# Small transfers of softmax statistics and weights: issued by GpSimd in place of SyncE

## The chip, the core and the metric

The kernel runs on one core of a Trainium2 chip. The core has five engines with an instruction queue each: TensorE (PE; its weight loads are shown as PEld), VectorE (DVE), ScalarE (ACT), GpSimd (POOL) and SyncE (SP). Every queue is worked off in order. A DMA is an instruction in the queue of some engine; it waits there for its semaphores like any other instruction, and the transfer itself is done by the core's 16 DMA engines. The metric is the device time of one execution in microseconds.

## What is computed

One layer of an encoder trunk on 1024 positions of width 1024, in float32. From the reference, cut to the part around the change:

```
hn = rms_norm(h, mix_norm_g);  proj = hn @ w_in            # q, k, v, glu, q_mem
q, k = partial_rotary(rms_norm(q)), partial_rotary(rms_norm(k))      # 8 heads x 64
for window, dil in ((128, 1), (512, 4), (2048, 16)):
    o, lse = dilated_attention(q, k, v, window, dil)
wts  = softmax(stack(lses), axis=0)
attn = sum(wts * stack(outs))
c    = silu(layer_norm(depthwise_conv31(ga * sigmoid(gg))))
mo   = cross-attention into 256 memory tokens, 4 heads x 64
h    = h + concat(attn, c, mo) @ w_out
f    = depthwise_conv3(rms_norm(h, ffn_norm_g) @ w_up);  h = h + (silu(fg) * fu) @ w_down
```

## The kernel before

Products are taken in three passes of a float32 value split into a rounded part and a rest (`w_hi`, `w_lo`), so every weight tile costs ACT a copy and POOL or DVE a subtraction (L636, L1208). The program has three stages: projections of x by `w_in` (L917, L943) with attention started beside them; the output projection by `w_out` (L1099) beside the last heads and the memory attention; and the feed-forward part (L1226, L1334). The projections come in the order q0 kv g0 g1 v0 q1 v1 q2 m q3; a projected tile of q and k is normalised and turned on POOL (`r` at L164 and L165, `t` and `raw` at L854 to L857) through four `raw` buffers.

Patterns two and three of the attention are one masked product, so a head has two groups: group 0 (window 128) and group 1 (the two dilated ones). For each head, `scores_of` (L239, L240) leaves in `stat` and `stat2` a negated maximum and a denominator for each query. Group 1 has its queries in another order, by residue class. `softmax_weights(h, ...)` brings both into one order and makes the weights of the two groups:

- L299: eight DMAs store `stat2` in scratch memory `st_d[h]`, 16 partitions of 4 pieces of 16 bytes each;
- L303, L304, L306: four DMAs load it back into `stat` in group 0's order;
- L315 to L326: POOL makes the weights `w` (ACT the exponential), TensorE turns them (L330), DVE copies them to `rows` (L333);
- L336, L337: four DMAs store `rows` in scratch memory `w_d[h]`.

`weigh(p)`, one for each pair of heads, loads each head's weights broadcast over 64 partitions into `wt` (L468, eight DMAs per pair, two `wt` buffers) and multiplies them onto the heads' outputs `u` (L480, L485). That is 20 DMAs per head and 160 in all. The values of a head are loaded at L393 and L394 into `v`, the new output's operands at L1085, projection weights at L595 and L603 (`w_raw`, two buffers, freed by the subtraction at L636).

The Python generators only say in which order work may be considered; the order on each engine is written by the scheduler of the tile framework, which plans with estimated times of its own. So an instruction that changes its engine also changes the place of others.

Of the kernel before, what the change touches and what calls it, by code (L numbers as in the profile page):

```python
# [18 lines left out]
S, D = 1024, 1024  # L19
# [113 lines left out]
def block(tc, a, out):  # L133
    nc = tc.nc
    pe, act, dve, pool, sp = nc.tensor, nc.scalar, nc.vector, nc.gpsimd, nc.sync
# [40 lines left out]
    st_d = [dpool.tile([8, 64, 2, 2], F, name=f"st_d{h}") for h in range(8)]  # L176
    w_d = [dpool.tile([1, 2, S + 64], F, name=f"w_d{h}") for h in range(8)]
    stored = {}

    def count(key):  # L180
        stored[key] = stored.get(key, 0) + 1
# [38 lines left out]
    def new_mixed(k):  # L220
        while not room_for(k):
            yield
        kind_of[k] = room_for(k)
        return (yield from st.several(2, kind_of[k], [128, S], R))

    def finish_mixed(k, parts):
        if kind_of[k] == "mx_part":
            for i, t in enumerate(parts):
                sp.dma_start(m_d[:, k, i], f32(t))
            st.free("mx_part", "mx_part")  # L230
            del kind_of[k]
            count(("mixed", k))
        else:
            mixed[k] = parts
# [54 lines left out]
    def split_mixed(k, parts, src, cut=slice(None)):  # L289
        hi, lo = (t[:, cut] for t in parts)  # L290
        act.activation(natural(hi), classed(src), AF.Copy)
        yield
        dve.tensor_tensor(natural(lo), classed(src), f32(natural(hi)), OP.subtract)

    def softmax_weights(h, stat, stat2):


        for k in range(8):
            sp.dma_start(st_d[h][k].rearrange("(r s) c n -> s r (c n)", r=4),  # L299
                         stat2[16 * k : 16 * k + 16].rearrange("s r c n -> s r (c n)"))  # L300
        yield
        there = stat[:, 1].rearrange("p u c n -> p u (c n)")
        sp.dma_start(there[0:64], st_d[h][1:8:2].rearrange("k p c n -> p k (c n)"))  # L303
        sp.dma_start(there[64:128, 0:3], st_d[h][2:7:2].rearrange("k p c n -> p k (c n)"))  # L304
        for c in range(2):
            sp.dma_start(stat[64:128, 1, 3, c], st_d[h][0, :, 1 - c])  # L306
        st.free("stat2")
        for _ in range(4):
            yield
        w = yield from st.new("w", [128, 2, 2, 4])  # L310
        wd = yield from st.new("wd", [128, 4, 2, 4])
        nm, d = (stat[:, :, :, :, i].rearrange("p g u c -> p g c u") for i in range(2))
        one = wd[:, 2]
        for g in range(2):
            pool.tensor_tensor(w[:, g], nm[:, g], nm[:, 1 - g], OP.subtract)  # L315
        yield
        act.activation(w, w, AF.Relu)
        act.activation(w, w, AF.Exp, scale=-1.0)
        yield
        for g in range(2):  # L320
            pool.tensor_tensor(wd[:, g], w[:, g], d[:, g], OP.mult)
        pool.tensor_tensor(one, wd[:, 0], wd[:, 1], OP.add)
        pool.tensor_tensor(wd[:, 3], one, expo[:, 0:1, None].to_broadcast([128, 2, 4]), OP.pow)
        pool.tensor_tensor(wd[:, 3], wd[:, 3], wd[:, 3], OP.mult)
        for g in range(2):
            pool.tensor_tensor(w[:, g], w[:, g], wd[:, 3], OP.mult)  # L326
        st.free("stat", "wd")
        yield
        ps = yield from st.new("z", [128, 512])
        pe.transpose(ps[0:16, 0:128], w.rearrange("p g c u -> p (g c u)"), ident)  # L330
        yield
        rows = yield from st.new("rows", [16, 128])
        dve.tensor_copy(rows, ps[0:16, 0:128])  # L333
        st.free("z", "w", "rows")
        for g in range(2):
            sp.dma_start(w_d[h][0, g, 64 : S + 64].rearrange("(u p) -> u p", p=128), rows[8 * g : 8 * g + 8])  # L336
            sp.dma_start(w_d[h][:, g, 0:64], rows[8 * g + 7 : 8 * g + 8, 64:128])  # L337
        count(("w", h))

    def head(h):  # L340
# [44 lines left out]
        else:  # L385
            st.kept["qk"] = 0
        st.start(softmax_weights(h, stat, stat2))
        while stored.get(("v", h // 4), 0) < NT:
            yield
# [66 lines left out]
    def weigh(p):  # L456

        for h in (2 * p, 2 * p + 1):
            while stored.get(("w", h), 0) < 1:
                yield  # L460
        parts = yield from new_mixed(p)
        wts = {}

        def fetch(half, g):

            t = wts[half, g] = yield from st.new("wt", [128, 512])
            for o in range(2):
                sp.dma_start(t[64 * o : 64 * o + 64],  # L468
                             w_d[2 * p + o][:, g, 512 * half : 512 * half + 512].to_broadcast([64, 512]))

        for g in range(2):
            yield from fetch(0, g)
        while stored.get(("u", 2 * p + 1), 0) < 4 or stored[("u", 2 * p)] < 4:
            yield
        us = joined[p]
        for half in range(2):
            cut = slice(512 * half, 512 * half + 512)
            adder = dve if p == 3 and half else pool
            for g in range(2):
                adder.tensor_tensor(us[g][:, cut], us[g][:, cut], wts[half, g], OP.mult)  # L480
                st.free("wt")
            if not half:
                for g in range(2):
                    yield from fetch(1, g)
            adder.tensor_tensor(us[0][:, cut], us[0][:, cut], us[1][:, cut], OP.add)  # L485
            yield
            yield from split_mixed(p, parts, us[0][:, cut], cut)
        st.free("u", "u")
        yield
        finish_mixed(p, parts)  # L490
# [834 lines left out]
    for part in range(2):  # L1325
        banks = [psp.tile([128, 512], F, name="ps_dn", tag=tag, bufs=n) for tag, n in DBANKS]
        for k in range(NF):
# [3 lines left out]
            for n, ps in enumerate(banks):  # L1331
                t, half = n // 2, n % 2
# [3 lines left out]
        for n, ps in enumerate(banks):  # L1336
            t, half = 4 * part + n // 2, n % 2
            r = pu.tile([128, 512], F, name="res", tag="part", bufs=6)
# [28 lines left out]
```

## Time and profile before

| what | value |
|---|---|
| median of 3 runs | 1310.53 us (1309.65 to 1312.85) |
| profiled execution, its own time | 1310.28 us |
| its span | 1308.5 us |
| mean granted TensorE clock | 0.963 |
| engine that is busy most | TensorE 91% |
| DMA queues | one hardware queue, 166460 packets, 163.63 MB, 40.3% of 16 engines |

The profile gives busy times of an engine, which do not count DMA-issuing instructions; these stand in rows of the queue (SPq, POOLq). "A <- B" in a row of waits reads: A stood idle until B was done. The chain of waits follows the execution back from its last instruction, at each step to what released it.

### The profile page before, as it was taken

What the parts mean: (1) busy time and instruction counts of PE and PEld (TensorE: products, weight loads), DVE (VectorE), ACT (ScalarE), POOL (GpSimd) and SP (SyncE); (2) the same over time, 40 slices, a digit from 0 to 9 for tenths busy, and PEclk for the clock granted to TensorE, in tenths of its full rate; (3) what the DMA queues carried; (4) which work ended last, traced back from release to release, by engine and by line L of the source; (5) the groups of instructions that cost most, each with busy time, mean ns of one, the idle gap of its engine ahead of it and who ended that gap; (6) DMA issues with size and microseconds to landing.
All of it is one profiled execution on the core that took longest, in us unless ns stands there. A gap on an engine that the chain in (4) does not pass through costs nothing.

```text
span 1308.5 us, 18556 instructions
## 1 busy us (share of the span) xinstructions
PE 1197.1 (91%) x6287; PEld 1000.3 (76%) x6287; DVE 868.7 (66%) x1272; ACT 626.6 (48%) x1296; POOL 788.5 (60%) x793
## 2 busy tenths in 40 slices
PE   4899988799988898885999999999999999999997
PEld 3887887799877786563877777777777788888886
DVE  6748879676685786887487778778787762224222
ACT  5664165468766576553344444344444443333331
POOL 4835286498894454367466667676676745555552
PEclk9999988999989898896999999999999999999999
DMA  7353525566575622161122222222222254448443
GB/s 253 112 170 100 159 82 161 169 180 178 144 252 164 188 74 78 28 213 49 34 87 81 65 86 67 81 89 65 89 71 83 81 175 155 145 145 272 146 146 120
DMA packets 166555, 164.81 MB, mean 126 GB/s; under 512 B 20322, under 2 KB 125756, under 8 KB 166460
## 3 DMA queue, kind: packets, MB, share of 16 engines
q1 hardware_dynamic: 166460, 163.63, 40.3%
q8 instruction: 49, 0.80, 0.3%
q14 instruction: 46, 0.38, 0.1%
HBM read 121.51 MB, written 42.08 MB: 125 GB/s over the span
## 4 chain that ended last, share of the span: by engine, by line
PE 46%; DVE 18%; issue 8%; ACT 7%; POOL 6%; DMA 5%; SPq 1%; POOLq 0%; ACTq 0%; DVEq 0%
PE ps_dn L1334 18%; PE ps_c L1226 6%; PE ps_d L1226 6%; PE proj L1099 4%; PE proj L917 3%; DVE yg L1295 3%; DVE conv L980 2%; DVE yu L1295 2%; PE o L287 2%; DMA v<-vr_d 2%; POOL up_lo L1208 2%; PE turn L278 2%; PE ps_a L1226 2%; ACT yu L1293 2%; DVE yg L1294 1%
## 5 line engine op out<-in xcount | busy, mean ns | idle before, releaser
L917 PE MATMUL proj<-w_hi,hnT 128*128 128x256 f32 x896 | 188.1, 298 | 23.7 <-ACT raw L832 12.9
L1208 POOL TENSOR_TENSOR up_lo<-dn_raw,up_hi 128x512 fp32r<-128x512 f32 x88 | 131.7, 1517 | 114.1 <-ACT up_hi L1207 111.3
L1208 POOL TENSOR_TENSOR up_lo<-up_sum,up_hi 128x512 fp32r<-128x512 f32 x88 | 154.8, 1768 | 55.8 <-PE ps_c L1226 22.7
L917 PEld LDWEIGHTS proj<-w_hi,hnT 128*128 128x128 f32 x896 | 150.9, 200 | 27.9 <-ACT raw L832 14.1
L1208 POOL TENSOR_TENSOR up_lo<-up_raw,up_hi 128x512 fp32r<-128x512 f32 x66 | 116.0, 1760 | 68.8 <-PE ps_a L1226 46.3
L1208 DVE TENSOR_TENSOR up_lo<-dn_raw,up_hi 128x512 fp32r<-128x512 f32 x44 | 57.6, 1311 | 147.5 <-ACT up_hi L1207 141.4
L1207 ACT ACTIVATE up_hi<-dn_raw 128x512 fp32r<-128x512 f32 x132 | 75.1, 623 | 161.4 <-issue 118.8
L1334 PE MATMUL ps_dn<-up_lo,up_hi 128*128 128x512 f32 x352 | 136.8, 389 | 0.0
L1334 PE MATMUL ps_dn<-up_hi,up_lo 128*128 128x512 f32 x352 | 136.3, 389 | 0.0
L1334 PE MATMUL ps_dn<-up_hi 128*128 128x512 f32 x352 | 134.7, 389 | 0.0
L917 PE MATMUL proj<-w_lo,hnT 128*128 128x256 f32 x448 | 131.9, 294 | 0.0
L1226 PE MATMUL ps_c<-S,up_hi 128*128 128x512 f32 x352 | 113.5, 404 | 6.6 <-ACT p L1278 6.6
L1226 PE MATMUL ps_a<-A,up_hi 128*128 128x512 f32 x352 | 111.1, 396 | 0.0
L636 POOL TENSOR_TENSOR w_lo<-w_raw,w_hi 128x512 fp32r<-128x512 f32 x44 | 62.8, 1437 | 59.4 <-ACT w_hi L634 58.8
L1221 DVE TENSOR_TENSOR up_sum<-up_raw,up_sum 128x512 f32<-128x512 f32 x40 | 59.0, 1476 | 50.4 <-POOL up_lo L1208 50.4
L917 PEld LDWEIGHTS proj<-w_lo,hnT 128*128 128x128 f32 x448 | 89.7, 200 | 0.5 <-POOL w_lo L624 0.4
L980 DVE SCALAR_TENSOR_TENSOR conv<-conv,cwT 128x1009 f32<-128x1009 f32 (+14 forms) x60 | 89.3, 1488 | 0.8
L1226 PEld LDWEIGHTS ps_c<-S,up_hi 128*128 128x128 f32 x352 | 65.4, 190 | 28.3 <-ACT p L1278 13.6
L1111 DVE TENSOR_TENSOR x<-proj,x 128x512 f32<-128x512 f32 x96 | 64.1, 682 | 25.0 <-PE proj L1099 24.9
L1293 ACT ACTIVATE yu<-cu,fwT 128x1024 f32<-128x1024 f32 x22 | 27.4, 1244 | 108.0 <-DVE cu L1286 106.3
L1226 PEld LDWEIGHTS ps_a<-A,up_hi 128*128 128x128 f32 x352 | 65.8, 188 | 15.8
L1334 PEld LDWEIGHTS ps_dn<-up_lo,up_hi 128*128 128x128 f32 x352 | 66.1, 188 | 13.8
(240 smaller groups left out, 3150.2 us busy)
## 6 DMA issues: line engine op xcount, KB each, us to landing
up_raw<-w_up SPq DMA_DIRECT2D x92, 256.0 KB
dn_raw<-w_down SPq DMA_DIRECT2D x88, 256.0 KB
g_d<-yg SPq DMA_DIRECT2D x22, 512.0 KB
dn_raw<-g_d SPq DMA_DIRECT2D x44, 256.0 KB
x<-x SPq DMA_DIRECT2D x16, 512.0 KB
qk_d<-out SPq DMA_DIRECT2D x32, 256.0 KB
qk<-qk_d SPq DMA_DIRECT2D x16, 512.0 KB
w_raw<-w_in SPq DMA_DIRECT2D x40, 128.0 KB
```

The source lines that it names most:

```text
L636: (dve if next(chunk_no) < EARLY else pool).tensor_tensor(lo, raw, f32(hi), OP.subtract)
L917: pe.matmul(ps[:, :256], lhs[i][:, k], c.parts[k][j], start=(k == 0 and i == 0 and j == 0), stop=(k == KT - 1 and i == 1))
L980: dve.scalar_tensor_tensor(acc[:, c0:c1], conv_in[i][:, c0 + k - 15 : c1 + k - 15], w, acc[:, c0:c1], OP.mult, OP.add)
L1099: pe.matmul(ps, mixed[k][i][:, 128 * t : 128 * t + 128], wo[k, half][j], start=(n == 0), stop=(n == 3 * len(ks) - 1))
L1111: dve.tensor_tensor(dst, ps, dst, OP.add)
L1207: act.activation(hi, src, AF.Copy)
L1208: adder.tensor_tensor(lo, src, f32(hi), OP.subtract)
L1221: adder.tensor_tensor(t, x, y, OP.subtract)
L1226: pe.matmul(ps, w[i][:, k], ops[x][j][:, k], start=(first and n == 0), stop=(n == 3 * KH - 1), skip_group_check=not first)
L1293: act.activation(y, c, AF.Identity, scale=tap[1], bias=b)
L1295: dve.scalar_tensor_tensor(y[:, 0 : S - 1], c[:, 1:S], tap[2], y[:, 0 : S - 1], OP.mult, OP.add)
L1334: pe.matmul(ps, gk[i][:, 128 * t : 128 * t + 128], wk[half][j], start=(k == 0 and m == 0), stop=(k == NF - 1 and m == 2))
```

## The change

Every DMA of `softmax_weights` and those of `fetch` in `weigh` are issued by POOL (`pool.dma_start`) in place of SP:

```
         for k in range(8):
-            sp.dma_start(st_d[h][k].rearrange("(r s) c n -> s r (c n)", r=4),
+            pool.dma_start(st_d[h][k].rearrange("(r s) c n -> s r (c n)", r=4),
                          stat2[16 * k : 16 * k + 16].rearrange("s r c n -> s r (c n)"))
         yield
         there = stat[:, 1].rearrange("p u c n -> p u (c n)")
-        sp.dma_start(there[0:64], st_d[h][1:8:2].rearrange("k p c n -> p k (c n)"))
-        sp.dma_start(there[64:128, 0:3], st_d[h][2:7:2].rearrange("k p c n -> p k (c n)"))
+        pool.dma_start(there[0:64], st_d[h][1:8:2].rearrange("k p c n -> p k (c n)"))
+        pool.dma_start(there[64:128, 0:3], st_d[h][2:7:2].rearrange("k p c n -> p k (c n)"))
         for c in range(2):
-            sp.dma_start(stat[64:128, 1, 3, c], st_d[h][0, :, 1 - c])
+            pool.dma_start(stat[64:128, 1, 3, c], st_d[h][0, :, 1 - c])
...
         for g in range(2):
-            sp.dma_start(w_d[h][0, g, 64 : S + 64].rearrange("(u p) -> u p", p=128), rows[8 * g : 8 * g + 8])
-            sp.dma_start(w_d[h][:, g, 0:64], rows[8 * g + 7 : 8 * g + 8, 64:128])
+            pool.dma_start(w_d[h][0, g, 64 : S + 64].rearrange("(u p) -> u p", p=128), rows[8 * g : 8 * g + 8])
+            pool.dma_start(w_d[h][:, g, 0:64], rows[8 * g + 7 : 8 * g + 8, 64:128])
...
             for o in range(2):
-                sp.dma_start(t[64 * o : 64 * o + 64],
+                pool.dma_start(t[64 * o : 64 * o + 64],
                              w_d[2 * p + o][:, g, 512 * half : 512 * half + 512].to_broadcast([64, 512]))
```

How it moves instructions shows at two places. The first is POOL's queue at the start of projection q2, where head 2's statistics (`st_d_80`) come back and pair 0's weights (`w_d_86`, `w_d_87`) are loaded. Before, from the turned tile `t_3102` to the power for `r_3071`:

```order
L856 TENSOR_TENSOR raw<-t_3102,t_3103 128x4x8
L857 TENSOR_TENSOR raw<-t_3102,t_3103 128x4x8
L164 TENSOR_SCALAR r_3071<-s_3070 128x4
L480 TENSOR_TENSOR u<-u,wt 128x512
L485 TENSOR_TENSOR u<-u 128x512
L854 TENSOR_TENSOR t_3168<-raw,rot_c 128x64
L854 TENSOR_TENSOR t_3169<-raw,rot_s 128x64
L165 TENSOR_TENSOR r_3071<-r_3071,expo 128x4
```

and in the changed program, from the same neighbourhood to the same power:

```order
L480 TENSOR_TENSOR u<-u,wt 128x512
L306 DMA stat<-st_d_80 64x2
L164 TENSOR_SCALAR r_3143<-s_3142 128x4
L306 DMA stat<-st_d_80 64x2
L856 TENSOR_TENSOR raw<-t_3102,t_3103 128x4x8
L857 TENSOR_TENSOR raw<-t_3102,t_3103 128x4x8
L304 DMA stat<-st_d_80 64x3x4
L468 DMA wt<-w_d_86 64x512
L468 DMA wt<-w_d_87 64x512
L303 DMA stat<-st_d_80 64x4x4
L165 TENSOR_TENSOR r_3071<-r_3071,expo 128x4
```

The loads of the statistics and of the weights now stand between the projection's own steps, two of them ahead of `raw` and four ahead of the power.

The second place is SP's queue around the load of the values `v` for head 6 (`st_d_84` are head 6's statistics). Before:

```order
L468 DMA wt<-w_d_90 64x512
L468 DMA wt<-w_d_91 64x512
L299 DMA st_d_84<-stat_5641 16x4x4 x6
L393 DMA v<-v_d_71 128x8x128
L394 DMA v<-vr_d_73 128x8x128
L346 DMA qk<-qk_d_69 128x1024
```

and in the changed program:

```order
L501 DMA km<-km_d 64x256
L503 DMA vm<-vm_d 128x2x128 x3
L393 DMA v<-v_d_71 128x8x128
L394 DMA v<-vr_d_73 128x8x128
L346 DMA qk<-qk_d_69 128x1024
```

The loads of weights and the stores of statistics that stood ahead of the `v` load are gone from this queue.

## The prediction

> **What bounds the kernel now.** I read the page first, then the busy times by stretch, then the chain of waits and the timelines of the two queues that exchange work.
>
> ```profile
> PE 1197.1 (91%) x6287; PEld 1000.3 (76%) x6287; DVE 868.7 (66%) x1272; ACT 626.6 (48%) x1296; POOL 788.5 (60%) x793
> ```
>
> This is the page's row for the whole span: TensorE is the bound on average. The busy times of three stretches of the attention stage, in which all moved transfers lie, show more; after the length they give PE, PEld, DVE, ACT and POOL, each with its count.
>
> ```profile
> 85.00:250.00 165.00, 145.21 (x1019) 135.17 (x1019) 132.29 (x210) 77.24 (x190) 88.00 (x103) 0.95 0.45 131
> 250.00:365.00 115.00, 103.26 (x828) 99.58 (x827) 74.31 (x193) 81.55 (x225) 95.76 (x158) 0.96 0.59 170
> 365.00:550.00 185.00, 161.37 (x892) 130.98 (x890) 139.11 (x346) 122.62 (x313) 96.25 (x147) 0.92 0.44 130
> ```
>
> The average of 60% for POOL hides that it is busy 95.76 of 115 us between 250 and 365 us, where heads 2 to 4 run beside the last three projections. Before and after that it is about half idle (88.00 of 165, 96.25 of 185). What POOL lacks in the middle stretch is this:
>
> ```profile
> POOL u L480 <- DMA wt<-w_d: 6.8, 1, 6.8
> POOL r L164 <- DVE s L838: 4.1, 4, 1.6
> POOL u L419 <- ACT u L415: 3.6, 2, 1.9
> ...
> POOL qe L353 <- PE turn L1009: 0.2, 1, 0.2
> ```
>
> These are POOL's waits from 250 to 365 us (total, times, longest). They and 115 - 95.76 = 19.2 us tell the same: 19.2 us is all the room there is. The chain of waits confirms it; from 263.5 to 290 us it runs on POOL almost without a break:
>
> ```profile
> 263.58 0.20 POOL r L164
> 263.86 0.72 POOL u L480
> ...
> 278.23 1.01 POOL qk L356
> ...
> 288.28 1.42 POOL w_lo L636
> ```
>
> So in this stretch a microsecond more on POOL is a microsecond on the path, and it is here that TensorE cannot hide it: it is itself busy 103.26 of 115.
>
> **The change part by part.** It moves 20 DMAs per head, 160 in all, from SP's queue to POOL's, and a planner places them anew among POOL's instructions. Nothing is computed more or less, and the bytes are the same. On SP their issue took (ns, least, median, most):
>
> ```profile
> L299 SPq DMA_DIRECT2D st_d<-stat x64: 302/424/1416, 97.7 to 477.1; - x64
> L306 SPq DMA_DIRECT2D stat<-st_d x16: 450/589/636, 101.3 to 475.8; - x16
> L304 SPq DMA_DIRECT2D stat<-st_d x8: 582/610/1579, 102.2 to 478.1; - x8
> L303 SPq DMA_DIRECT2D stat<-st_d x8: 591/605/2127, 102.9 to 481.5; - x8
> L468 SPq DMA_DIRECT2D wt<-w_d x32: 444/518/1608, 123.3 to 528.0; - x32
> L336 SPq DMA_DIRECT2D w_d<-rows x16: 263/269/495, 121.8 to 508.7; - x16
> L337 SPq DMA_DIRECT2D w_d<-rows x16: 214/249/253, 122.2 to 509.0; - x16
> ```
>
> By medians that is 64 x 0.424 + 16 x 0.589 + 8 x 0.610 + 8 x 0.605 + 32 x 0.518 + 16 x 0.269 + 16 x 0.249 = 71 us, or 0.44 us each, taken from SP.
>
> *Price of one on POOL.* No row shows a DMA issued by POOL. The low end is SP's 0.44 us (it cannot be a gain: an instruction on POOL takes time). The high end is the slowest thing that POOL does on a tile this small:
>
> ```profile
> L165 POOL TENSOR_TENSOR r<-r,expo 128x4 f32<-128x4 f32 x32 | 35.8, 1121 | 0.9
> L323 POOL TENSOR_TENSOR wd<-wd,expo 128x8 f32<-128x8 f32 x8 | 14.2, 1777 | 0.4
> L315 POOL TENSOR_TENSOR w<-stat 128x8 f32<-128x8 f32 x16 | 3.4, 227 | 7.1 <-DVE hl L866 6.4 <-DVE stat L239 0.6
> ```
>
> A subtraction of 128x8 takes 0.23 us, a power of the same size 1.78 us: the time goes by work per element, not by bytes. A transfer in 64 pieces (16 partitions of 4) is such work per piece. I take 1.0 us, near the power on 128x4 (1.12 us) and about the middle of 0.44 and 1.78, and keep both ends.
>
> The Trainium skill gives two figures for this and they pull apart. Its page "DMA: Bandwidth & Descriptors", section "Latency and other measured facts", puts the first byte of a DMA issued by GpSimd at about 1 us against 0.6 us from SP; an estimate from it is 1 us per DMA and the same sum as mine. The same page, section "Anatomy of one DMA — SWDGE (gpsimd) path", calls the generation of descriptors "small, variable" beside a dispatch of about 50 ns; by that the estimate would be about 0.1 us each, 56 x 0.1 = 6 us in the full stretch, and no overflow at all. No run here shows either yet; the second speaks for the faster rival below.
>
> *Stretch 250 to 365 us.* By their neighbours, 36 of the 160 stand ahead of it, 56 in it (16 with head 2's statistics and pair 0's weights, 18 and 18 with the heads after, 4 of pair 1's weights) and 68 behind. POOL would have 95.8 + 56 x 1.0 = 151.8 us of work for 115 us: 36.8 us over, called +37. Nine of the 56 stand inside the POOL chain of 263 to 290 us itself. With 0.44 us the overflow is 24.6 - 19.2 = +5; with 1.78 us it is 99.7 - 19.2 = +80. At 1.0 us nothing covers it: what waits behind is the projections' own work (r, t and raw at L164, L165, L854 to L857), whose four `raw` buffers hold TensorE back a few tiles later.
>
> *Ahead of it*, 88.0 + 36 = 124 of 165 us: hidden, cost 0, in POOL's idle 77 us; at 1.78 us it is 152, still under 165. *Behind it*, 96.3 + 68 = 164 of 185 us: the sum fits, cost 0; at 1.78 us it would be 217, or +32.
>
> *Waits that come along.* A DMA in POOL's queue holds all that stands behind it. SP paid this for the moved transfers:
>
> ```profile
> SPq L336 <- DVE rows L333: 25.5, 4, 16.1
> SPq L299 <- ACT prob L240: 8.6, 4, 5.2
> SPq L468 <- DMA w_d<-rows: 5.7, 5, 3.2
> SPq L303 <- DMA st_d<-stat: 3.9, 3, 2.7
> ```
>
> That is 43.7 us over eight heads; 56/160 of it, 15 us, falls into the full stretch, and as the planner puts other POOL work between the steps I charge a third: +5 (bounds 0 and +15). Behind such a wait stand the projections' r and raw, for which DVE and then TensorE wait.
>
> *What SP gains.* SP's queue is in order too, and the loads of the values `v` stand behind moved transfers. Head 6, then head 5:
>
> ```profile
> 434.42 1.15 PE L287 MATMUL o<-pt,v 128*128 128x256 f32 x9
> 440.04 1.09 SPq L468 DMA_DIRECT2D wt<-w_d  x2
> 441.66 3.69 SPq L299 DMA_DIRECT2D st_d<-stat  x6
> 445.44 0.38 SPq L393 DMA_DIRECT2D v<-v_d  x1
> 383.19 9.24 SPq L299 DMA_DIRECT2D st_d<-stat  x8
> 401.13 0.42 SPq L393 DMA_DIRECT2D v<-v_d  x1
> ```
>
> and, in the chain of waits, the load that follows:
>
> ```profile
> 445.92 7.02 DMA v<-vr_d
> ```
>
> The last product that read the old `v` of head 5 ended at 435.6; the load for head 6 left SP at 445.4, after transfers that now go elsewhere. Up to 10 us earlier there, and about as much at head 5 behind the 9.24 us of `st_d`. But what can be won is TensorE's idle time there:
>
> ```profile
> 390.00:455.00 65.00, 56.16 (x318) 46.22 (x316) 43.14 (x95) 41.17 (x93) 29.74 (x36) 0.97 0.60 169
> 455.00:520.00 65.00, 58.86 (x334) 48.47 (x333) 49.87 (x143) 44.39 (x127) 33.47 (x56) 0.92 0.32 85
> ```
>
> 130 - 115.0 = 15 us at most. I take 7, about half, since after the `v` load comes the next limit, VectorE's adds of the output projection.
>
> The last moved transfer starts at 528.0 us (row L468); the feed-forward part behind it has none: 0. Sum: +37 + 5 - 7 = +35. The profiled execution took 1310.28 us (span 1308.5), so 1345; the median of the runs before, 1310.53, is the same within 0.3 us.
>
> **The rivals.**
>
> *Faster: SP's relief wins (1300).* Place: the `v` loads of heads 5 and 6, 401 to 453 us. Price: -15 from the rows above, +5 for POOL at SP's own 0.44 us. It decides as soon as 56 x price - 19.2 is under 15, a price under 0.61 us; for a gain over 0.3% (4 us) under 0.54 us. For it speaks that the chain runs over DMA v<-vr_d for 7.02 us; against it, that POOL does small tiles in software times of 0.2 to 1.8 us.
>
> *Hidden (1311).* Price near 0.6 us: overflow 56 x 0.6 - 19.2 = 14, relief -14. Only a balance by chance gives it.
>
> *Slower a little (1321).* POOL at SP's price, +5, and the in-order waits, +5, with no relief because the planner leaves the `v` load behind loads of `w_raw`, which wait for POOL.
>
> *Much slower (1395).* VectorE holds POOL up while POOL writes the transfers. That such a thing exists is in the timelines:
>
> ```profile
> 260.88 2.29 DVE L980 SCALAR_TENSOR_TENSOR conv<-conv,cwT 128x1010 f32<-128x1010 f32 x1
> 262.06 1.22 POOL L856 TENSOR_TENSOR raw<-t,t 128x32 f32<-128x32 f32 x1
> 271.33 0.30 POOL L856 TENSOR_TENSOR raw<-t,t 128x32 f32<-128x32 f32 x1
> ```
>
> The same instruction takes 1.22 us under a VectorE operation with two inputs from SBUF and 0.30 us without: 0.9 us of hold. With half of the DMAs held, a mean price of 1.0 + 0.45, and with the full 15 us of waits: 56 x 1.45 - 19.2 + 15 = +77, and some of the 68 behind no longer fit: 1395. Against it: the long convolution steps end where the full stretch has hardly begun, at 264.5 us, and after them VectorE's operations of this kind are short:
>
> ```profile
> L980 DVE SCALAR_TENSOR_TENSOR conv<-conv,cwT x60: 1255/1276/2397, 108.5 to 264.5; 128x1009 f32<-128x1009 f32 x4, 128x1010 f32<-128x1010 f32 x4, 128x1011 f32<-128x1011 f32 x4, 128x1012 f32<-128x1012 f32 x4
> ```
>
> The Trainium skill has the rule on its page "SBUF — State Buffer", section "SBUF: two separate sides", in "The 'DVE blocks DMA' trap": while VectorE holds the port pair that it shares with GpSimd, GpSimd cannot write descriptors and the transfer starves. The two rows on L856 agree in kind for arithmetic; none here shows it for a DMA.
>
> **How the numbers follow.** Forecast (price 0.8 to 1.3 us, 1325 to 1372, centre 1345): 0.55. Much slower: 0.18. Faster: 0.11. Hidden: 0.08. A little slower: 0.08. The measurement tells 0.3%, about 4 us, from no change. Faster 0.11, same 0.08, slower 0.55 + 0.18 + 0.08 = 0.81. The range 1302 to 1395 leaves out about half of the faster case and half of the much slower one, 0.15 together.
>
> **What would show it.** Right: rows of POOL's queue for L299 at about 1 us; POOL without idle time from 250 to over 390 us; waits of TensorE or VectorE for POOL's r, raw or qk that are not there now; the whole feed-forward part some 35 us later, at its old pace; the `v` loads of heads 5 and 6 sooner after the last product of the head before. Wrong: DMA rows of POOL under 0.5 us, or POOL's arithmetic running on beside them; or a POOL queue that stands in waits for `st_d` and `rows`, which would put the cost in the waits and not in the issue.

## The result, and the profile after

The changed kernel took 1370.13 us in the median of 4 runs (1360.61 to 1371.22), the kernel before 1310.09 us in 4 runs beside it (1307.16 to 1312.85). The ratio is 1.0443 (95% interval 1.0391 to 1.0495): 58 us slower. Below, a cost in microseconds is always (ratio - 1) x 1311. The profiled execution took 1370.61 us, its span 1368.8 us.

The page's row for the whole span, after:

```profile
PE 1224.6 (89%) x6287; PEld 1021.3 (75%) x6287; DVE 868.6 (63%) x1272; ACT 632.6 (46%) x1298; POOL 875.4 (64%) x953
```

POOL is busy 86.9 us longer (788.5 before) and has 160 instructions more; DVE and ACT do what they did. DMAs in POOL's queue are counted as busy time, so the 86.9 us are their issue. By line, between 85 and 620 us (count, then busy us and mean ns, then the idle time ahead of them and what ended it):

```profile
L299 POOL DMA_DIRECT2D st_d<-stat x64 | 33.0, 523 | 2.0 <-ACT prob L240 1.9
L468 POOL DMA_DIRECT2D wt<-w_d x32 | 17.6, 551 | 3.1 <-PE s L258 1.1 <-POOL u L480 0.9 <-DMA w_d<-rows 0.8
L306 POOL DMA_DIRECT2D stat<-st_d x16 | 8.9, 557 | 3.3 <-DMA st_d<-stat 3.1
L336 POOL DMA_DIRECT2D w_d<-rows x16 | 8.9, 555 | 8.7 <-DVE rows L333 8.7
L337 POOL DMA_DIRECT2D w_d<-rows x16 | 8.4, 527 | 0.0
L304 POOL DMA_DIRECT2D stat<-st_d x8 | 5.3, 668 | 2.2 <-DMA st_d<-stat 2.2
L303 POOL DMA_DIRECT2D stat<-st_d x8 | 5.3, 658 | 0.1
```

Together 87.4 us, 0.55 us for each DMA (SP: 0.44), and 19.4 us of waits that they brought into the queue. The stretches of the attention stage (length, then PE, PEld, DVE, ACT and POOL busy with counts):

```profile
85.00:250.00 165.00, 142.04 (x947) 129.96 (x945) 133.03 (x193) 74.32 (x176) 101.36 (x126) 0.93 0.44 125
250.00:365.00 115.00, 94.95 (x725) 93.03 (x725) 52.68 (x151) 69.50 (x188) 99.41 (x169) 0.91 0.46 137
365.00:550.00 185.00, 150.13 (x837) 123.36 (x835) 118.73 (x302) 103.92 (x273) 133.31 (x224) 0.90 0.49 141
```

From 250 to 365 us POOL is only 3.7 us busier than before (99.41 against 95.76), although it now also issues DMAs; TensorE does 725 products in place of 828. So less work gets done in the same time. The same 6287 products also keep TensorE busy 27.5 us longer over the whole span (1224.6 against 1197.1), at a mean granted clock of 0.948 against 0.963. In the runs below that lost 20 us or more the clock was 0.942 to 0.959, in the executions of the kernel before beside them 0.959 to 0.968; no run separates what the slower products cost from the waits beside which they stand. The loss can be dated from the first and last products of two lines (the last two times are the first and the last start). The projections before, then after:

```profile
L917 PE MATMUL proj<-w_hi,hnT x896: 274/283/582, 16.4 to 370.6; 128*128 128x256 f32 x180
```
```profile
L917 PE MATMUL proj<-w_hi,hnT x896: 274/283/583, 17.0 to 404.4; 128*128 128x256 f32 x180
```

Before, the last projection product started at 370.6 us, after at 404.4: 34 us late. The first product of the feed-forward part (L1226) started at 579.0 and at 640.5 us: 62 us late, and the end is 60.3 us late. So about 34 us are lost by the end of the projections, 28 us between there and the feed-forward part, and nothing in that part.

The chain of waits shows the DMAs at the place whose order was printed above (start, length, what):

```profile
273.42 0.20 POOL r L164
273.70 1.29 POOL u L480
274.99 0.52 POOL stat L306
...
276.92 0.57 POOL stat L304
277.49 0.42 POOL wt L468
...
278.54 0.62 POOL stat L303
279.17 1.06 POOL r L165
280.25 0.44 DVE raw L860
```

Between the two halves of `r_3071`, 0.20 us and 1.06 us long, lie 5.5 us, and 3.2 us of them are DMAs of other steps (L306 twice, 0.52 and 0.58 us, L304, L468 twice, L303); DVE, then ACT and TensorE, stand behind.

### The profile page after: what moved, and what is told of

Its sections match the earlier page's. It is cut to its first block, busy times and chain, and to the rows that moved or that the text cites. A ratio compares the mean times of both kernels' runs of the same rounds, so it can differ in the third digit from the quotient of the medians.

```text
span 1368.8 us, 18618 instructions
## 1 busy us (share of the span) xinstructions
PE 1224.6 (89%) x6287; PEld 1021.3 (75%) x6287; DVE 868.6 (63%) x1272; ACT 632.6 (46%) x1298; POOL 875.4 (64%) x953
## 3 DMA queue, kind: packets, MB, share of 16 engines
q0 software_dynamic: 5632, 4.41, 1.3%
## 4 chain that ended last, share of the span: by engine, by line
PE 47%; DVE 17%; DMA 11%; ACT 8%; POOL 8%; issue 7%; SPq 1%; POOLq 0%; ACTq 0%; DVEq 0%
PE ps_dn L1334 15%; PE ps_c L1226 7%; PE ps_d L1226 6%; PE proj L917 6%; PE proj L1099 3%; PE ps_a L1226 2%; DMA w_raw<-w_in 2%; DVE yg L1295 2%; PE o L287 2%; DVE conv L980 2%; POOL up_lo L1208 2%; DMA qk<-qk_d 2%; DVE yu L1295 2%; PE ps_b L1226 2%; ACT prob L240 1%
## 5 line engine op out<-in xcount | busy, mean ns | idle before, releaser
L917 PE MATMUL proj<-w_hi,hnT 128*128 128x256 f32 x896 | 193.9, 307 | 21.2 <-DVE out L886 8.0
L917 PEld LDWEIGHTS proj<-w_hi,hnT 128*128 128x128 f32 x896 | 157.8, 210 | 25.5 <-ACT raw L832 7.0
L917 PE MATMUL proj<-w_lo,hnT 128*128 128x256 f32 x448 | 135.7, 303 | 0.5 <-POOL w_lo L624 0.5
L1226 PE MATMUL ps_c<-S,up_hi 128*128 128x512 f32 x352 | 114.1, 405 | 6.1 <-ACT p L1278 6.1
L1226 PE MATMUL ps_a<-A,up_hi 128*128 128x512 f32 x352 | 111.1, 396 | 0.0
L917 PEld LDWEIGHTS proj<-w_lo,hnT 128*128 128x128 f32 x448 | 94.2, 210 | 1.0 <-POOL w_lo L624 0.9
L1226 PEld LDWEIGHTS ps_c<-S,up_hi 128*128 128x128 f32 x352 | 65.9, 191 | 27.5 <-ACT p L1278 12.6
L1226 PEld LDWEIGHTS ps_a<-A,up_hi 128*128 128x128 f32 x352 | 65.8, 188 | 15.7
L240 ACT ACTIVATE prob<-prob,stat 128x256 f32<-128x256 f32 x128 | 63.6, 501 | 27.7 <-DVE stat L239 27.5
```

What stands on the lines that cost most here:

```text
L240: act.activation(t, t, AF.Exp, bias=nm, scale=-1.0, accum_out=den)
L917: pe.matmul(ps[:, :256], lhs[i][:, k], c.parts[k][j], start=(k == 0 and i == 0 and j == 0), stop=(k == KT - 1 and i == 1))
L1226: pe.matmul(ps, w[i][:, k], ops[x][j][:, k], start=(first and n == 0), stop=(n == 3 * KH - 1), skip_group_check=not first)
```

## The experiments

**The theories.** A: the DMAs cost what POOL loses by them, either by the time it issues them (A1, occupancy) or by the waits that come into its queue and the later landing (A2). B: the planner's new order on all queues costs, since loads now stand behind stores that wait for late POOL work. C: the old order is a lucky or picked one and any other is worse.

To hold an order, ordering edges without semaphores chain the instructions of each engine in the sequence of a table; the run under "Is it any other order?" is held in the same way and loses nothing, so the edges themselves cost no time that shows:

```
-        block(tc, aps, out)
+        block(tc, aps, out); issue_in_order(tc, nc)
...
+    for n in np.cumsum(steps.astype(np.int64)).tolist():
+        i = traced[n]
+        if n in FREE: continue
+        if i.engine in last:
+            tc.add_manual_dep(i, last[i.engine], kind, reason="order")
+        last[i.engine] = i.name
```

### Order against engine

First the changed kernel's DMAs in the old order (`ORDER_TABLE` of the kernel before, `FREE` the 160 DMAs):

> All 160 DMAs are issued by POOL, as in the changed kernel, but every other instruction of every engine is held in the order that it has in the kernel before (manual ordering edges without semaphores); only the 160 are placed freely. Theory A, occupancy and in-order waits: POOL pays 87 us of issue (0.55 us each) and the waits in its queue, whatever the order around them; the time stays near that of the changed kernel, 1355 to 1375. Theory B, the re-planned order: most of the 60 us comes from the planner's new order on the queues (loads of v, qk and w_raw behind stores that wait for late POOL work); with the old order only the overflow of the full stretch is left, 56 x 0.55 - 19.2 = 12 us less what SP gains: 1305 to 1330.

Then the reverse, the kernel before with the changed kernel's table:

> The 160 DMAs stay with SP, as before, but every other instruction of every engine is held in the order that the planner wrote for the changed kernel. Theory A, occupancy and in-order waits on POOL: without the DMAs on POOL nothing is lost, 1305 to 1320. Theory B, the re-planned order: the order costs by itself, 1340 to 1370, and the old order's loss on POOL of the first run and this one together make about the 60 us.

Measured: 1371.14 us, ratio 1.0437 (1.0403 to 1.0472), and 1364.24 us, ratio 1.0391 (1.0352 to 1.0431). Each part alone costs nearly the whole, 57 and 51 us, and both together 58. So theory A was right on the first run and missed the second, and theory B the other way round. In the old order the cost shows as waits for POOL: who waited for it from 250 to 430 us (total, times, longest),

```profile
DVE raw L860 <- POOL r L165: 23.9, 6, 12.5
ACT mx_part L291 <- POOL u L485: 22.9, 3, 15.2
...
DVE s L838 <- POOL r L164: 12.2, 2, 8.8
```

and in the kernel before, in the same window:

```profile
DVE raw L860 <- POOL r L165: 4.5, 5, 1.9
...
ACT mx_part L291 <- POOL u L485: 1.9, 3, 1.0
```

In the changed kernel itself, in the same window, the first of these rows has grown far less:

```profile
DVE raw L860 <- POOL r L165: 8.6, 5, 4.0
```

There the other engines follow an order in which they stand less behind POOL and are no faster for it. The second run shows that this order costs by itself:

```profile
250.00:365.00 115.00, 94.18 (x724) 92.08 (x723) 57.19 (x158) 69.12 (x191) 74.94 (x127) 0.90 0.45 131
```

POOL is relieved, 74.94 us busy where the changed kernel has 99.41, and yet TensorE does 724 products, one fewer than there. So an order planned for POOL as the planner estimated it keeps the slow pace when POOL is relieved, and the two 50s are not two causes that add up. The reading that fits both runs is that the one is the loss and the other its imprint on the plan; which places of that order lose the time no run shows.

### Is it any other order?

The kernel before, with the table that the planner writes when its estimate for a DMA on SP is 615 in place of 625 ns:

> The kernel before with all DMAs on SP; only the order differs: it is the one that the planner writes when its estimate for a DMA on SP is lowered by 10 of 625 ns. Nothing on the chip has another price. Theory C, tuning: the order of the kernel before is a picked one, any other costs tens of microseconds: 1325 to 1365. Theory B, the order matters only as it follows POOL's lateness: 1305 to 1318.

1311.43 us, ratio 0.9979 (0.9955 to 1.0002): no loss. By the two traces at least 1185 of TensorE's 6287 places hold a product of another line or tile, and it does not matter. Theory C fell, as far as one other order can tell.

### The planner's price

The changed kernel in the order that results from a lower estimate for POOL's DMAs:

> The changed kernel, all 160 DMAs on POOL, in the order that the planner writes when its own estimate for the issue of a DMA on POOL is lowered from 0.99 to 0.45 us, near the 0.55 us measured (0.44 us was SP's). Theory B, the order: part of the 60 us comes from planning with the wrong price, and 1325 to 1350 results. Theory A, occupancy: the work on POOL is the same, and the time stays at 1360 to 1375. Theory C, tuning: any order other than the one of the kernel before is worse, since that one was picked for this program; the result lies anywhere from 1335 to 1375, whatever the price.

1348.43 us, ratio 1.0292 (1.0267 to 1.0317), 38 us. So some 20 us of the changed kernel's 58 go with an order planned with nearly twice the measured price; 38 us stay with an order planned near it (0.45 against 0.55 us). Theory A missed here, and B's and C's ranges both hold the result; C fell by the run before. With one order for each price, the 20 us are what these two orders differ by, and not a proof that the price alone makes them.

### Occupancy or waits

Spare work in POOL's queue at the places of the DMAs, while SP issues them:

```
+    def after_spare(*move): pool.tensor_tensor(spare, half, half, OP.mult); pool.tensor_tensor(spare, half, half, OP.mult); sp.dma_start(*move)
...
-            sp.dma_start(st_d[h][k].rearrange("(r s) c n -> s r (c n)", r=4),
+            after_spare(st_d[h][k].rearrange("(r s) c n -> s r (c n)", r=4),
```

> The kernel before, every instruction in its old order and all DMAs on SP; ahead of no DMA anything waits anew. Added are 320 spare multiplications of 128x12 on POOL, two (estimated at 0.25 us each from L315, 0.23 us on 128x8) at each of the 160 places where POOL issues a DMA in the first run; they read a constant and nobody reads them. So POOL loses about the issue time of the DMAs, but waits for nothing and SP keeps its queue. If POOL's lost time is the cost (theory A1, occupancy): 1355 to 1370. If it is the waits that the DMAs bring into POOL's queue, and their later landing (theory A2): 1312 to 1330.

1361.27 us, ratio 1.0390 (1.0365 to 1.0415), 51 us. The spare row, between the first and the last of its 320:

```profile
L166 POOL TENSOR_TENSOR spare<-expo 128x12 f32<-128x12 f32 x320 | 83.0, 259 | 22.7
```

83.0 us of work that nobody needs, against 87 us of DMA issue, reproduces 51 of the 57 us. By the two traces POOL carries out the same sequence as in the first run, with two spare instructions in the place of each DMA. A1 holds: time taken on POOL is enough to make nearly the whole loss in the old order. What is left for the DMAs' waits, their landing and SP's relief together is 6 us, with intervals that touch; it isn't resolved.

### Which DMAs cost

Two kernels with one kind each on POOL, in the order that the planner writes for each (the edit is the change's own, of the lines named):

> Only the statistics' DMAs (L299, L303, L304, L306; 96 of the 160, 52.5 of the 87.4 us of issue in the changed kernel) go to POOL; the weights' stay with SP; the planner writes the order anew. If the cost goes by issue time on POOL, 52.5/87.4 of 60 us: 1346. If it goes by the waits in the queue (about 7 of the 17 us that the moved DMAs wait on POOL are the statistics'), 1335. If the order decides, no rule gives the number; it may be anything from 1305 to 1370, and not the sum with the next run.

> Only the weights' DMAs (L336, L337, L468; 64 of the 160, 34.9 of the 87.4 us of issue) go to POOL; the statistics' stay with SP; the planner writes the order anew. By issue time 34.9/87.4 of 60 us: 1334, and this gain over the kernel before plus that of the run before make 60. By order: anything from 1305 to 1370, not additive.

1341.98 us, ratio 1.0219 (1.0189 to 1.0249), 29 us; and 1333.66 us, ratio 1.0149 (1.0119 to 1.0178), 20 us. They stand 60 to 40, as the issue times do (52.5 to 34.9), and sum to 48 of 58. Both orders were planned anew, so this agrees with a cost by issue time and doesn't prove it.

Then three kernels by place, in the old order, for instance

```
-            sp.dma_start(st_d[h][k].rearrange("(r s) c n -> s r (c n)", r=4),
+            (pool if h in (2, 3, 4) else sp).dma_start(st_d[h][k].rearrange("(r s) c n -> s r (c n)", r=4),
```

> Old order on every engine; only the 36 DMAs ahead of 250 us go to POOL (statistics and weights' stores of heads 0 and 1, the first half of pair 0's weights). The prediction hides them at cost 0: 1308 to 1315. If the costs of the three groups add up to that of all 160 in the old order: 59 - 30.2 - 19.5 = 9, so 1320.

> Old order on every engine; only the 56 DMAs that the prediction placed in the stretch from 250 to 365 us go to POOL (statistics of heads 2 to 4, weights' stores of heads 2 and 3, weights' loads of the second half of pair 0 and of pair 1); 104 stay with SP. If the cost arises in the full stretch alone, as the prediction has it: 1360 to 1370. If every DMA costs alike wherever it stands: 56/160 of 59 us, 1333. If only the overflow of 56 x 0.55 - 19.2 us: 1324.

> Old order on every engine; only the 68 DMAs behind the stretch go to POOL (statistics of heads 5 to 7, weights' stores of heads 4 to 7, weights' loads of pairs 2 and 3). The prediction hides them at cost 0: 1308 to 1315. If every DMA costs alike: 68/160 of 59 us, 1337.

| on POOL | ratio (95%) | us | per DMA |
|---|---|---|---|
| 36 ahead of 250 us | 1.0022 (1.0002 to 1.0041) | 3 | 0.08 |
| 56 in the full stretch | 1.0239 (1.0215 to 1.0263) | 31 | 0.56 |
| 68 behind it | 1.0143 (1.0107 to 1.0178) | 19 | 0.28 |

The medians were 1318.75, 1341.47 and 1330.76 us, beside 1313.65, 1311.25 and 1311.25 us of the kernel before. None of the three values stated for the middle group (1324, 1333, 1360 to 1370) came out, and the late group lies between its two. The sum is 53 of the 57 us that all 160 cost in the old order. In the full stretch the loss is as large as the whole issue time, 56 x 0.55 us. With the 56 DMAs the stretch grows from 115 to about 146 us:

```profile
250.00:396.00 146.00, 112.90 (x833) 108.59 (x832) 73.79 (x198) 81.52 (x225) 121.21 (x211) 0.88 0.48 137
```

TensorE gets through 833 products in it, about the 828 of before, but they keep it busy 112.90 us in place of 103.26, at a granted clock of 0.88 in place of 0.96. POOL stands idle for 146 - 121.21 = 24.8 us in it, where it stood 19.2 us before. The 31 us are thus 25.4 us of busy time (30.8 us of DMAs, less 5.4 us by which POOL's other work was shorter) and 5.6 us more of idle time. From 250 to 396 us POOL waits for much the same as before, and for some rows of the DMAs themselves (4.1 us in six rows, of which the largest is the last one shown):

```profile
POOL u L480 <- DMA wt<-w_d: 9.5, 2, 7.7
POOL u L419 <- ACT u L415: 5.0, 2, 3.1
POOL r L164 <- DVE s L838: 2.7, 3, 1.6
POOL stat L304 <- DMA st_d<-stat: 2.3, 1, 2.3
```

Behind the stretch, from 365 to 560 us of the run with the 68 DMAs, other engines wait longer for POOL. TensorE waits for `w`, which it must turn; the kernel before has no such row there:

```profile
PE z L330 <- POOL w L326: 10.6, 2, 5.3
```

ACT waits for `u` (L413) for 4.8 us, where it waited 1.1 us before.

### Another engine

The 160 DMAs issued by ScalarE (`act.dma_start`), in the old order and in the planner's own:

> Old order on every engine; the 160 DMAs go to ScalarE's queue in place of POOL's. ACT is busy 81.55 of the 115 us between 250 and 365 us, POOL 95.76. Theory A1 in the form that the runs so far give it (time on an engine of the projections' chain is lost in full in the middle stretch, about half elsewhere): with SP's price of 0.44 us, 56 x 0.44 = 25 in the stretch and about 0.25 x 104 = 26 elsewhere, 1350 to 1365. If a queue's spare time does cover issue (my prediction's way of reckoning), 33 us of room holds 25: 1305 to 1315.

> The 160 DMAs on ScalarE's queue, in the order that the planner writes for it. Theory A1: about as with the old order, 1335 to 1365. If ACT's spare time covers the issue and SP gains: 1300 to 1315.

1334.82 us, ratio 1.0146 (1.0113 to 1.0179), 19 us; and 1323.87 us, ratio 1.0067 (1.0042 to 1.0092), 9 us. Both expectations missed: ACT does not lose all that it issues, nor are its idle times enough to hide it. Issue in ACT's queue, ns (least, median, most):

```profile
L299 ACTq DMA_DIRECT2D st_d<-stat x64: 309/386/1782, 98.1 to 499.6; - x64
```
```profile
L468 ACTq DMA_DIRECT2D wt<-w_d x32: 452/470/612, 125.9 to 553.5; - x32
```

By the medians of its seven lines that is 67 us, 0.42 each, of which 19 us come out at the end, against 57 of 87 us on POOL. No version with moved DMAs beat the kernel before: of the three queues SP, which computes nothing, was the place where these DMAs held up least.

## Why the prediction was right or wrong

The direction, the resource and the stage were right: POOL's time between 250 and 365 us is on the path, and there is a loss. The size was not: +35 forecast, +58 measured, and the sum's terms were off by more than the total. That 1370 us lies inside the forecast's 1325 to 1372 is luck: that range stood for a price of 0.8 to 1.3 us, and the price measured 0.55. By the prediction's own rule a price under 0.61 us decides for the faster rival (1300). Of its signs, the feed-forward part came later at its old pace (62 us, not 35), and there are longer or new waits for POOL's `r` and `qk`; L299 at 1 us and a POOL without idle time did not come, and of the two `v` loads only that of head 6 came sooner.

*Price of one, 1.0 us.* It measured 0.55 us. The power on 128x4 (1.12 us) was the wrong neighbour, and so was the idea of work for each piece: 64 pieces of 16 bytes take 523 ns at L299, 256 such pieces 658 ns at L303, and 64 rows of 2 KB 551 ns at L468. SP's 0.44 us was the near row. The Trainium skill's page "DMA: Bandwidth & Descriptors", section "Latency and other measured facts", with its 1 us to the first byte speaks of another thing than what POOL loses; the 0.55 us measured lies about halfway between the two estimates that were made from that page.

*The room of 19.2 us.* This is the step that failed. The prediction read POOL's idle time as room that a DMA fills before it costs anything, although its own reading of the chain, that in this stretch a microsecond more on POOL is a microsecond on the path, leaves no such room. With the 0.55 us put into its formula, 56 x 0.55 - 19.2, the stretch would lose 12 us; it lost 31, as much as all of 56 x 0.55. The idle time did not fill: it was there again, 24.8 us, in the longer stretch. The likely reason lies in what the waits are, though no run follows them one by one. POOL waits there for a DVE result `s`, an ACT result `u` and a transfer `wt` that themselves follow earlier work of POOL's or of engines that wait for POOL, so they should arrive later by what POOL is later. The rows quoted under "what POOL lacks" named these waits; they should have been read as part of the chain and not as a reserve. That +37 came out near 31 is two errors that cancel, a price of twice the true one and a room that isn't.

*Behind it, cost 0.* Mis-sized: 19 us. 96.3 + 68 = 164 of 185 us does fit on average, but about half of the issue time (19 of the 37 us that the 68 take) came out at the end. The rows above put TensorE at `w` and ACT at `u` behind POOL there; which of these waits made the 19 us no run separates. *Ahead of it, cost 0:* 3 us, right.

*Waits that come along, +5, and SP's gain, -7.* The waits in the DMAs' rows are 19.4 us over all heads, and 4.1 us in the full stretch of the run with the 56, near the +5. Their cost, together with the relief of SP, is at most some 6 us net, which no run separates. Part of the relief did occur, at head 6. In the changed kernel, the last products of heads 4 and 5 with `v`,

```profile
448.12 0.31 PE L287 MATMUL o<-pt,v 128*128 128x128 f32 x1
...
485.94 0.57 PE L287 MATMUL o<-pt,v 128*128 128x256 f32 x4
```

and on SP the loads of `v` for heads 5 and 6:

```profile
448.73 0.62 SPq L393 DMA_DIRECT2D v<-v_d  x1
...
474.67 5.70 SPq L503 DMA_DIRECT2D vm<-vm_d  x3
481.44 0.36 SPq L393 DMA_DIRECT2D v<-v_d  x1
```

The load for head 5 left SP 0.3 us after head 4's last product ended; before, it left at 401.1 us, ahead of that product's end (404.8 us), though it stood behind 9.24 us of `st_d`. The load for head 6 left 5 us ahead of the end of head 5's last product, behind loads for the memory heads; before, it left 9.9 us after it (445.4 against 435.6 us). So the prediction's 10 us at head 6 were there, and those at head 5 were not. No run shows time won by it.

*What had no term.* The planner's own price. Some 20 us of the 58 go with an order planned for DMAs of 0.99 us. The prediction had the planner's order only as a small rival, with `v` loads left behind `w_raw` loads (1321); the kind of cause was right there, the size was not, and the place stays open.

*The much slower rival* asked for VectorE to hold POOL while it writes transfers. Eleven of the 160 DMAs were issued under one of VectorE's long convolution steps, and they took 547 ns in the median, the other 149 took 529. Two places, DMA and step (start, length, what; a row of several holds them one behind the other):

```profile
111.12 0.66 POOL L303 DMA_DIRECT2D stat<-st_d  x1
...
138.56 1.07 POOL L468 DMA_DIRECT2D wt<-w_d  x2
```
```profile
109.60 7.48 DVE L980 SCALAR_TENSOR_TENSOR conv<-conv,cwT 128x1009 f32<-128x1009 f32 x4
...
134.86 4.84 DVE L980 SCALAR_TENSOR_TENSOR conv<-conv,cwT 128x1023 f32<-128x1023 f32 x2
```

0.66 and twice 0.53 us, as elsewhere: the hold of 0.9 us that arithmetic on POOL showed is not there for issuing a DMA. Nor did those transfers land later: from issue to landing the eleven took 2.7 us in the median, the other 149 took 2.9. The Trainium skill's "DVE blocks DMA" trap, on its page "SBUF — State Buffer", is stated for VectorE operations in a two-port mode. These convolution steps are operations with two inputs, so these rows do not show whether the trap holds.

## What to carry to other kernels

Idle time of an engine inside a loop of engines that wait for each other need not be room: a wait that depends on the engine's own earlier work can move along when work is added. Here added time counted in full where POOL's work was on the chain, about half behind that stretch, and hardly at all ahead of it. Price it at the nearest row of the same kind (a DMA on another queue), then test with spare work of the same length, which separates occupancy from the waits and the landing of the moved instructions. And when a scheduler writes the order, its estimate of the moved instruction is part of the change.

## What the runs showed of the hardware

A plain DMA issued by GpSimd occupies it for 0.51 to 0.79 us, with little regard to its pieces and bytes; ScalarE's and SyncE's queues spend 0.25 to 0.62 us, by the medians of the lines, and more where there are more pieces (0.27 us for the 8 rows of L336, 0.61 us for the 256 pieces of L303, on both). The page lists POOL's DMAs in a queue of their own, as 5632 packets of 4.41 MB; before, the same bytes were 13088 packets of the hardware queue. From issue to landing the stores and loads of `st_d` took 1.6 to 8.0 us on POOL (median 3.0). A tiny POOL multiplication (128x12) takes 0.26 us, so two of them take about as much of POOL's time as one DMA.
